# Full-row second products in two attentions, and an SSM's output products grouped by rows

## The chip, the cores and the metric

The kernel runs on one core of one Trainium2 chip, as one program with one launch. The metric is the device time of an execution in microseconds. Before the change it is 1551.39 us, the median of three runs from 1551.03 to 1553.93. A measurement of this kernel can tell apart some 0.2%.

The core has five engines with a queue each: TensorE (PE in the profile, its weight loads apart as PEld), VectorE (DVE), ScalarE (ACT), GpSimd (POOL) and SyncE (SP, which here only starts transfers). Each runs its instructions in the order in which they were issued and waits at an instruction until the semaphores of its operands are there.

## The reference, cut to what matters

Two transformer-like blocks run on one sequence of 512 tokens with 1024 channels, in float32. Block 1 has NSA attention (8 heads of 64, two groups of keys), MLA attention and an MLP, all modulated by a vector c. Block 2 has a state space model (SSM) on 512 channels, a second attention of 8 heads of 64 on the other 512, and a gated MLP.

The change touches three places of it:

```python
# NSA, selected and windowed keys; chunked_attention has the same product
s = jnp.einsum('bghqd,bgqkd->bghqk', qq, k_sel).astype(jnp.float32) * scale - slopes * dist_s[:, :, None]
p = masked_softmax(s, smask[:, :, None])
...
scores = jnp.einsum('bnqhd,bnkhd->bhnqk', qc, kb).astype(jnp.float32) / math.sqrt(HEAD_DIM)
...
# SSM
_, states = lax.associative_scan(combine, (a, bu), axis=1)
y = jnp.einsum('bsgp,ghp->bsgh', states, c_mat).real + d_skip.astype(f32) * uf
```

Scores are sums over 64 head channels. SSM outputs are sums over 64 complex states of each of 32 groups.

## The kernel before, in words

**Order of the work.** The program isn't issued as it is written. `Rec` records every instruction of every engine with what it reads and writes (so every instruction has the source line 337, and names of tiles tell them apart). `Plan.schedule` (line 159) then plays the program through with estimated costs from `Plan.price` (line 121): each engine takes the instruction of the lowest number whose operands are there and for whose tiles there is a place. The order of planned starts is the order issued. For a float32r matmul the price is its columns over 2400 us (line 140); the rows it uses don't enter. `merge` runs several generators side by side by their costs, and each `yield` gives the cost of what was just recorded.

**Stages around the change.** NSA (`nsa_units`, from line 1527) is merged with the dense products of block 1's other inputs (line 1576). Later, `ssm(0)` is merged with dense products of block 2 (line 2053), and then `att2_stream`, `ssm(1)` and further dense products are merged (line 2054). Dense products have names like `mm<-hh,wh`: inputs and weights are each split into a high and a low float32r part, and three products (high-high, low-high, high-low) make one of full accuracy.

**Scores.** `Unit.qk` (class at line 1256) makes the scores of one head and one block of 128 queries, with 128, 256, 384 or 512 keys. `passes` gives two products that accumulate in one bank of PSUM. The first takes `qA` (128 rows: the high part of the query on 64 partitions, its low part on the other 64; even and odd heads have them the other way round) against `kA` (the high part of the key on both halves). The second takes the high part of the query alone, 64 rows, against the low part of the key:

```python
return [(qA[:, cs], kA[:, :n]), (qA[r:r + 64, cs], kL[r:r + 64, :n])]
```

It stands in line 1548 for NSA and in line 2027 for the second attention. NSA's `kL` is written on both halves of its partitions (`kskw`, line 786). In the second attention one tile `k2l` (line 1118, in `qk2_evac`) holds the low keys of two heads, one on each half. MLA has products with 96 rows, which the change doesn't touch.

**The SSM's outputs.** `ssm(hf)` (line 1905) treats half of the SSM's channels. It loads tables `rec` and inputs `U`, makes state products (`T<-U,rec`, 64 columns of the array each), rotates and scans on VectorE and GpSimd, which gives `st` (tiles `ss`: real and imaginary states), and then makes the outputs in lines 1961 to 1973. For each of two sets `o` and each half `e` of the partitions, four groups `k` have three float32 products that accumulate in `Y`: one with `U` (128 rows), one with the real and one with the imaginary states (`T<-ss,rec`, 64 rows, on the lower or the upper half of the partitions by `e`). The three follow each other, group by group. `Y` is a tile of the tag T, which has two places in PSUM (line 501); attention transposes use the same tag.

## Time and profile before

| What | Value |
|---|---|
| median of the runs | 1551.39 us (1551.03 to 1553.93) |
| profiled execution, first to last instruction | 1547.8 us (the profile has no other time of this execution) |
| TensorE busy | 1473.4 us, 95% of the span, 7008 records |
| TensorE weight loads busy | 1193.4 us, 77% |
| VectorE busy | 994.4 us, 64% |
| ScalarE busy | 627.0 us, 41% |
| GpSimd busy | 273.6 us, 18% |
| mean granted clock of TensorE | 0.970 |
| products `S<-kL,qA` / `S<-k2l,qA` / `T<-ss,rec`, 64 rows | 64 / 32 / 128 records |

How to read the profile: one execution is recorded on the chip. "A<-B,C" means an instruction that writes tile A and reads B and C, without buffer numbers; a shape like 64*128 ahead of the sizes is the rows and columns of TensorE's array that a product uses. Float32 products appear as two records each. Busy time of TensorE is the union of its matmuls, whose ends are modelled, so a busy TensorE need not be a fast one; the steps between starts tell more. The granted clock is the share of full speed that TensorE was given. The chain of waits is followed back from the last instruction to what released each step.

### The profile page before, as it was taken

To read this page: it belongs to the slowest core of one execution; us is meant where nothing else is said; L and a number is where in the kernel's file an instruction comes from. 1 tells how busy PE (TensorE), PEld (TensorE's weight loads), DVE (VectorE), ACT (ScalarE), POOL (GpSimd) and SP (SyncE) were. 2 spreads that over 40 slices of the span, in tenths; PEclk is the share of its full clock that TensorE was granted. 3 is DMA by queue.
4 is the path that set the end of the run, shared out by engine and by line. 5 is a ranking of instruction groups with operands and counts; after the bars stand their busy time and mean duration, and the time that the engine had idled before them with its cause. 6 is when DMAs were issued, how large, how long until landed. Compare 5 with 4: busy or idle time off the path is not lost.

```text
span 1547.8 us, 19040 instructions
## 1 busy us (share of the span) xinstructions
PE 1473.4 (95%) x7008; PEld 1193.4 (77%) x7008; DVE 994.4 (64%) x1972; ACT 627.0 (41%) x1057; POOL 273.6 (18%) x262
## 2 busy tenths in 40 slices
PE   4889999998899999999999998999899999999997
PEld 3687777786688888887787887877688888888885
DVE  7835687877997788766443556296876544553544
ACT  3425556665654342332323431274733322231222
POOL 7514040535200000000213111037031000000000
PEclk9998999999999999999999998699899999999998
DMA  9355252434026422333444665113122333333311
GB/s 368 110 181 173 68 168 84 137 109 170 28 94 202 128 76 89 109 105 126 132 146 160 218 225 109 41 56 116 51 93 82 97 108 90 101 95 110 104 60 55
DMA packets 72604, 184.75 MB, mean 119 GB/s; under 512 B 16792, under 2 KB 17640, under 8 KB 72512
## 3 DMA queue, kind: packets, MB, share of 16 engines
q1 hardware_dynamic: 63424, 158.62, 32.2%
q0 software_dynamic: 7552, 22.97, 4.4%
q10 hardware_dynamic: 1536, 1.95, 0.4%
q8 instruction: 55, 0.90, 0.2%
q14 instruction: 37, 0.30, 0.1%
HBM read 165.41 MB, written 19.67 MB: 120 GB/s over the span
## 4 chain that ended last, share of the span: by engine, by line
PE 78%; DVE 9%; issue 5%; DMA 4%; POOL 2%; ACT 2%; SPq 0%; DVEq 0%; POOLq 0%; ACTq 0%
PE mm L337 64%; PE T L337 7%; PE S L337 4%; PE O L337 3%; DVE sb L337 2%; DMA aw<-in_w_ada 2%; POOL aacg L337 1%; DMA adaw<-in_w_ada 1%; DVE wl L337 1%; DVE pl L337 1%; DVE zqd L337 1%; DMA U<-ud 1%; DVE q L337 1%; DVE sr L337 1%; DVE xt L337 0%
## 5 line engine op out<-in xcount | busy, mean ns | idle before, releaser
L337 PE MATMUL mm<-hh,wh 128*128 128x512 f32 x880 | 363.4, 415 | 13.3 <-ACT hh L337 5.8
L337 ACT CAST wh<-wr 128x1024 fp32r<-128x1024 f32 x209 | 219.2, 1051 | 366.1 <-PE mm L337 331.0
L337 PE MATMUL mm<-hl,wh 128*128 128x512 f32 x880 | 355.1, 403 | 0.2 <-DVE hl L337 0.2
L337 PE MATMUL mm<-hh,wl 128*128 128x512 f32 x880 | 352.8, 401 | 0.5 <-DVE wl L337 0.5
L337 DVE TENSOR_TENSOR wl<-wr,wh 128x1024 fp32r<-128x1024 f32 x199 | 256.3, 1289 | 144.8 <-ACT wh L337 142.3
L337 PEld LDWEIGHTS mm<-hh,wh 128*128 128x128 f32 x880 | 167.9, 192 | 52.6 <-ACT hh L337 6.6
L337 PEld LDWEIGHTS mm<-hh,wl 128*128 128x128 f32 x880 | 168.8, 192 | 37.7 <-issue 1.4
L337 PEld LDWEIGHTS mm<-hl,wh 128*128 128x128 f32 x880 | 169.2, 192 | 34.7 <-issue 2.4
L337 PE MATMUL mm<-fh,wl 128*128 128x512 f32 x416 | 162.5, 391 | 0.0
L337 PE MATMUL mm<-fl,wh 128*128 128x512 f32 x416 | 162.3, 390 | 0.0
L337 PE MATMUL mm<-fh,wh 128*128 128x512 f32 x416 | 161.7, 390 | 0.0
L337 PEld LDWEIGHTS mm<-fh,wh 128*128 128x128 f32 x416 | 78.1, 188 | 16.8 <-issue 0.6
L337 PEld LDWEIGHTS mm<-fh,wl 128*128 128x128 f32 x416 | 78.1, 188 | 16.8 <-issue 0.6
L337 PEld LDWEIGHTS mm<-fl,wh 128*128 128x128 f32 x416 | 78.1, 188 | 16.6 <-DVE PBr L337 0.2
L337 ACT ACTIVATE sb<-sb,st 128x256 f32<-128x256 f32 (+3 forms) x128 | 71.5, 560 | 47.4 <-DVE st L337 46.5
L337 POOL TENSOR_TENSOR adacc<-adacc,adaw 128x1024 f32<-128x1024 f32 x28 | 68.9, 2460 | 55.1 <-ACT adaw L337 54.6
L337 PE MATMUL T<-ident,sb 128*128 128x128 f32 x320 | 57.7, 280 | 11.1 <-DVE sb L337 6.0
L337 DVE TENSOR_TENSOR pl<-T,ph 128x384 fp32r<-128x384 f32 (+1 forms) x96 | 56.9, 595 | 16.5 <-ACT ph L337 13.6
L337 ACT CAST ph<-T 128x384 fp32r<-128x384 f32 (+1 forms) x96 | 49.0, 511 | 44.9 <-PE T L337 35.6
L337 POOL TENSOR_TENSOR st<-st,mhalf 128x1 f32<-128x1 f32 x4 | 2.2, 547 | 358.2 <-DVE st L337 358.2
L337 PEld LDWEIGHTS T<-ident,sb 128*128 128x128 f32 x320 | 40.3, 143 | 22.8 <-DVE pl L337 6.2
L337 DVE CUSTOM_DVE_ANT_0 sb<-S,nb 128x256 f32<-128x256 f32 (+2 forms) x96 | 45.3, 482 | 15.6 <-PE S L337 15.0
(373 smaller groups left out, 2560.4 us busy)
## 6 DMA issues: line engine op xcount, KB each, us to landing
wr<-in_w_fc SPq DMA_DIRECT2D x64, 512.0 KB, 3.6
wr<-in_w_in SPq DMA_DIRECT2D x48, 512.0 KB, 4.4
wr<-in_w_gu SPq DMA_DIRECT2D x44, 512.0 KB, 3.6
adaw<-in_w_ada POOLq DMA_DIRECT2D x32, 512.0 KB, 4.3
wr<-in_w_down SPq DMA_DIRECT2D x22, 512.0 KB, 3.5
aw<-in_w_ada SPq DMA_DIRECT2D x32, 256.0 KB, 6.0
wr<-in_w_out SPq DMA_DIRECT2D x16, 512.0 KB, 3.8
rec<-srec SPq DMA_DIRECT2D x28, 256.0 KB, 5.8
```

Source lines behind the costliest of these rows:

```text
L337: fn(*o.a, **o.kw)
```

## The change

The second score products of NSA and of the second attention use all 128 rows: `qA[:, cs]` against the whole `kL`. In NSA both halves of `kL` hold the key's low part, so the query's low part is now multiplied with it too. In the second attention each head gets a `k2l` tile of its own, whose other half is set to zero by GpSimd.

In `ssm`, both `Y` tiles of a set are made first. All eight products with `U` come first, then the products with the states, which alternate between the two halves of the partitions for each `k` and each of the real and imaginary parts. The first product with `U` in a bank now carries the start flag alone. Both copies to `ye` come at the end of the set. The costs that are yielded change from 0.65 per three products to 0.9 per four. Comments and docstrings of the file are gone too.

```diff
@@ qk2_evac
-                kl = slot(F32R, "k2l")
                 for e in range(2):
-                    kA = slot(F32R, "k2A")
+                    kA, kl = slot(F32R, "k2A"), slot(F32R, "k2l")
                     r, o = e * 64, (1 - e) * 64
+                    gp.memset(f(kl)[o:o + 64], 0.0)
                     act.copy(kA[r:r + 64], p[r:r + 64])
                     act.copy(kA[o:o + 64], p[r:r + 64])
                     later(dve.tensor_tensor, kl[r:r + 64], p[r:r + 64], f(kA)[r:r + 64], op=OP.subtract)
@@ nsa_units, and in the same way att2_units
-                    return [(qA[:, cs], kA[:, :n]), (qA[r:r + 64, cs], kL[r:r + 64, :n])]
+                    return [(qA[:, cs], kA[:, :n]), (qA[:, cs], kL[:, :n])]
@@ ssm
         for o in range(2):
             pcr, pci = rec[8 + o], rec[10 + o]
             sr, si = st[o]
+            Y = [bank("T")[:, 0:256].rearrange("p (g c) -> p g c", g=4) for e in range(2)]
             for e in range(2):
-                Y = bank("T")[:, 0:256].rearrange("p (g c) -> p g c", g=4)
-                r = slice(64 * e, 64 * e + 64)
                 for k in range(4):
                     g = 2 * k + e
-                    mm(Y[:, k], rec[2 * o + g // 4][:, 128 * (g % 4):128 * (g % 4) + 128], U[:, 8 * o + g], True, False)
-                    mm(Y[:, k], pcr[r, 128 * k:128 * k + 128], sr[r, k], False, False)
-                    mm(Y[:, k], pci[r, 128 * k:128 * k + 128], si[r, k], False, True)
-                    yield 0.65
-                act.copy(ye[:, 8 * o + e:8 * o + 8:2], Y)
+                    mm(Y[e][:, k], rec[2 * o + g // 4][:, 128 * (g % 4):128 * (g % 4) + 128], U[:, 8 * o + g], k == 0,
+                       False)
+                yield 0.9
+            for k in range(4):
+                for w, (pc, s_) in enumerate(((pcr, sr), (pci, si))):
+                    for e in range(2):
+                        r = slice(64 * e, 64 * e + 64)
+                        mm(Y[e][:, k], pc[r, 128 * k:128 * k + 128], s_[r, k], False, w == 1)
+                yield 0.9
+            for e in range(2):
+                act.copy(ye[:, 8 * o + e:8 * o + 8:2], Y[e])
```

TensorE's order is the same in both kernels up to SSM half 0, so in NSA only the rows of the second products change. In SSM half 0 the order before was this, behind the first wait for the states (`T_1898` and `T_1902` are the two banks, `ss` the states, `rec` the tables; each row is one product):

```order
L337 MATMUL T_1898<-ss_1883,rec_1867 128x64
L337 MATMUL mm_1896<-hh_1804,wh_1886 128x512
L337 MATMUL T_1898<-ss_1883,rec_1869 128x64
L337 MATMUL T_1898<-U_1873,rec_1859 128x64
L337 MATMUL T_1898<-ss_1883,rec_1867 128x64
L337 MATMUL T_1898<-ss_1883,rec_1869 128x64
L337 MATMUL T_1898<-U_1873,rec_1860 128x64
L337 MATMUL T_1898<-ss_1883,rec_1867 128x64
L337 MATMUL T_1898<-ss_1883,rec_1869 128x64
```

Now it is this at the same place (banks `T_1898` and `T_1899`):

```order
L337 MATMUL T_1899<-U_1873,rec_1859 128x64 x2
L337 MATMUL T_1899<-U_1873,rec_1860 128x64 x2
L337 MATMUL T_1899<-ss_1883,rec_1867 128x64
L337 MATMUL T_1899<-ss_1883,rec_1869 128x64
L337 MATMUL T_1898<-ss_1883,rec_1867 128x64
L337 MATMUL T_1899<-ss_1883,rec_1867 128x64
L337 MATMUL T_1898<-ss_1883,rec_1869 128x64
L337 MATMUL T_1899<-ss_1883,rec_1869 128x64
L337 MATMUL T_1898<-ss_1883,rec_1867 128x64
L337 MATMUL T_1899<-ss_1883,rec_1867 128x64
```

The products with `U` moved together ahead of those with the states, which stand in groups of one to ten between dense products; TensorE's whole order has 33 separate stretches of `T<-ss,rec` before (17 in half 0, 16 in half 1) and 17 now (7 and 10). In the second attention before, TensorE's order at the first head is:

```order
L337 MATMUL S_1928<-k2A_1916,qA_1906 128x512
L337 MATMUL S_1947<-k2A_1916,qA_1906 128x384
L337 MATMUL S_1950<-k2A_1916,qA_1906 128x256
L337 MATMUL mm_1946<-hh_1804,wh_1909 128x512
L337 MATMUL S_1928<-k2l_1915,qA_1906 128x512
L337 MATMUL S_1947<-k2l_1915,qA_1906 128x384
L337 MATMUL S_1950<-k2l_1915,qA_1906 128x256
L337 MATMUL mm_1946<-hl_1805,wh_1909 128x512
```

This piece didn't move; in the whole order the 32 products with `k2l` stand in 24 separate stretches before. On POOL the first two new clears stand here, between the clears of the SSM's state tiles (`ss`) and the bias tiles of the second attention (`nb`):

```order
L337 MEMSET ss_1883 128x512
L337 MEMSET ss_1894 128x512
L337 MEMSET k2l_1916 64x512
L337 MEMSET k2l_1918 64x512
L337 DMA nb_1415_1927<-es 128x256
L337 TENSOR_SCALAR nb_1415_1927<-vec 128x256
```

The other six stand further on, among the bias tiles and the rotations of SSM half 1. Four loads of `x2` for the next stage stand later in SP's order than before, among its weight loads.

## The prediction

> **What bounds the kernel now.** I read the page's chain first, then busy time by stage, then the chain inside each stage, then TensorE's timeline.

> ```profile
> PE 78%; DVE 9%; issue 5%; DMA 4%; POOL 2%; ACT 2%; SPq 0%; DVEq 0%; POOLq 0%; ACTq 0%
> ```

> TensorE makes 78% of the chain that ended last, so its time is the kernel's time wherever no other engine ends the wait. Busy time in the stages that the change touches (columns: stretch, its length, then PE, PEld, DVE, ACT, POOL with busy us and instructions, granted clock, DMA share, GB/s): NSA, SSM half 0, the second attention in two parts, its tail.

> ```profile
> 133.00:330.00 197.00, 193.83 (x933) 145.85 (x933) 148.41 (x357) 116.28 (x244) 59.76 (x47) 0.98 0.36 118
> 958.00:997.00 39.00, 38.35 (x124) 31.68 (x125) 9.82 (x25) 3.66 (x7) 2.04 (x3) 0.52 0.03 7
> 997.00:1045.00 48.00, 46.54 (x310) 37.36 (x309) 43.50 (x124) 34.07 (x72) 12.71 (x18) 1.00 0.26 75
> 1045.00:1100.00 55.00, 55.00 (x286) 43.40 (x284) 38.39 (x94) 27.99 (x59) 26.96 (x18) 1.00 0.36 115
> 1100.00:1117.00 17.00, 12.66 (x45) 9.78 (x46) 13.35 (x29) 14.15 (x29) 0.00 (x0) 0.70 0.00 0
> ```

> TensorE fills the first four. VectorE is nearly idle in SSM half 0, busy for three quarters of NSA, and close behind TensorE in 997 to 1045. No single engine fills the tail after 1100. The chain inside 133 to 330, 1000 to 1045 and 1045 to 1100, in this order:

> ```profile
> by line: PE mm L337 42.9%; PE S L337 16.6%; DVE sb L337 9.6%; PE T L337 9.2%; PE O L337 7.4%; issue 4.8%; DVE wl L337 2.4%; DVE pl L337 2.0%; ACT adaw L337 1.1%; ACT sb L337 0.9%; DVE onl L337 0.7%; DVE o L337 0.7%; DVE st L337 0.6%; ACT wh
> by line: PE mm L337 42.8%; PE S L337 15.9%; PE T L337 13.3%; DVE sr L337 8.2%; PE O L337 4.0%; DVE pl L337 3.8%; DVE qA L337 3.1%; DVE wl L337 2.7%; ACT ph L337 2.2%; DVE st L337 1.6%; DVE qk L337 1.3%; issue 0.8%; DVE sb L337 0.6%; ACTq L3
> by line: PE mm L337 51.1%; PE T L337 27.6%; PE S L337 12.8%; PE O L337 7.7%; ACT ph L337 0.9%; issue 0.0%
> ```

> TensorE's share is 42.9 + 16.6 + 9.2 + 7.4 = 76% in NSA, again 76% in the first part of the second attention, and 99% in its second part. I use these shares as the part of a TensorE saving that reaches the end.

> **What a 64-row product costs now.** Matmuls overlap, so a price is the step from one start to the next, not the duration. Two places in NSA (start, duration, instruction, rows * columns of the array):

> ```profile
> 299.87 0.28 PE L337 MATMUL S<-kA,qA 128*128 128x256 f32 x1
> 300.08 0.38 PE L337 MATMUL S<-kL,qA 64*128 64x256 f32 x1
> 300.39 0.50 PE L337 MATMUL mm<-hh,wh 128*128 128x512 f32 x1
> 300.73 0.40 PE L337 MATMUL mm<-hl,wh 128*128 128x512 f32 x1
> 300.96 0.39 PE L337 MATMUL mm<-hh,wl 128*128 128x512 f32 x1
> ...
> 303.72 0.22 PE L337 MATMUL S<-kA,qA 128*128 128x128 f32 x1
> 303.87 0.32 PE L337 MATMUL S<-kL,qA 64*128 64x128 f32 x1
> 304.12 0.50 PE L337 MATMUL mm<-hh,wh 128*128 128x512 f32 x1
> 304.46 0.40 PE L337 MATMUL mm<-hl,wh 128*128 128x512 f32 x1
> 304.70 0.39 PE L337 MATMUL mm<-hh,wl 128*128 128x512 f32 x1
> ```

> For comparison MLA's score products, which use 96 rows, and the weight loads of all 64 kL products:

> ```profile
> 384.52 0.28 PE L337 MATMUL S<-kmH,qml 96*128 96x256 f32 x1
> 384.64 0.28 PE L337 MATMUL S<-kmL,qmh 96*128 96x256 f32 x1
> 384.76 0.40 PE L337 MATMUL mm<-ch,wh 128*128 128x512 f32 x1
> L337 PEld LDWEIGHTS S<-kL,qA 64*128 64x128 f32 x64 | 12.0, 188 | 15.9 <-issue 15.0
> ```

> An undisturbed step is 0.12 us after 256 columns (384.52 to 384.64 to 384.76) and 0.23 us after 512 (300.73 to 300.96). Around kL three steps are long: into it 0.21 for 0.12, out of it 0.31 for 0.12, and the next dense step 0.34 for 0.23. From 299.87 to 300.96 that is 1.09 us where 0.12 + 0.12 + 0.23 + 0.23 = 0.70 would do: 0.39 us lost. At 128 columns, 303.72 to 304.70 takes 0.98 us where 0.11 + 0.11 + 0.23 + 0.23 = 0.68 would do (0.11 from the small products below): 0.30 lost. The load queue idles 15.9 us ahead of the 64 loads of kL, for nothing that is recorded: these loads don't run ahead. Products with 96 rows lose nothing. So it is the passage between half the array's rows and all of them that costs, not a short product as such.

> [...]

> **The sum.** *NSA scores.* 64 second products become full-row products like their kA partners. kL already holds the low part on both halves of its partitions, so nothing is added. At 0.37 us each (between 0.30 and 0.39, near the upper since three of four widths are 256 or more), 64 x 0.37 = 23.7 us of TensorE; by the 76% share 18 us. Bounds: 12, half of it, if VectorE's 148 us bind earlier; 24 if all of it counts.

> *Second attention.* 32 products; where three k2l products stand together they share a passage, so the order of TensorE's instructions has 24 passages: 24 x 0.37 = 8.9 us, half of it before 1045 (4.4 x 76% = 3.4), half after (4.4, less what falls near the tail: 4.0). Together 7.4, bounds 3 and 8.9. Added are four tiles and eight clears of 64x512 on POOL. The nearest clears, of 128x512:

> ```profile
> L337 POOL MEMSET ss<- x4: 522/526/528, 860.1 to 963.5; 128x512 f32 x4
> ```

> 8 x 0.53 = 4.2 us on an engine busy for 12.7 of 48 and 27 of 55 us. Queued behind them on POOL are the bias tiles and the SSM's rotations, and VectorE waits for both; the first two clears stand right behind two of the clears of this row, long before the attention. I take nothing, since POOL's own idle time covers them; uncovered they cost at most 4.2.

> *SSM output products.* Every fp32 product is two records. Half 1 runs at full clock in a regular period, and small full-row products stand early in the program:

> ```profile
> 1052.53 0.50 PE L337 MATMUL mm<-hh,wh 128*128 128x512 f32 x1
> 1052.86 0.39 PE L337 MATMUL mm<-hl,wh 128*128 128x512 f32 x1
> 1053.09 0.40 PE L337 MATMUL mm<-hh,wl 128*128 128x512 f32 x1
> 1053.33 0.33 PE L337 MATMUL T<-U,rec 128*128 128x64 f32 x2
> 1053.59 0.66 PE L337 MATMUL T<-ss,rec 64*128 64x64 f32 x4
> 1054.18 0.53 PE L337 MATMUL mm<-hh,wh 128*128 128x512 f32 x1
> ...
> 97.77 4.74 PE L337 MATMUL S<-fm,wr 128*128 128x62 f32 x41
> 102.34 0.61 PE L337 MATMUL S<-hs,vec 128*128 128x62 f32 x4
> ```

> Undisturbed records of that size step at (102.34 - 97.77) / 41 = 0.111 us. The period of 1.65 us should then be 3 x 0.23 + 6 x 0.111 = 1.36: a visit to 64 rows costs 0.29. Half 1 makes 16 visits, in the new order 10: 6 x 0.29 = 1.7 us. Half 0 runs at half clock (0.52 above):

> ```profile
> 958.65 0.43 PE L337 MATMUL T<-ss,rec 64*128 64x64 f32 x2 [3.94 <-DVE ss L337]
> 960.54 1.11 PE L337 MATMUL T<-ss,rec 64*128 64x64 f32 x4
> 962.20 1.11 PE L337 MATMUL T<-ss,rec 64*128 64x64 f32 x4
> 992.08 0.79 PE L337 MATMUL mm<-hh,wh 128*128 128x512 f32 x1
> ```

> One group takes 962.20 - 960.54 = 1.66 us; six records at half clock should take 6 x 0.222 = 1.33, so a visit costs 0.33. 17 visits become 7: 3.3 us. (Three U products move ahead of the wait of 3.94 us and three dense products behind it; 6 x 0.222 against 3 x 0.43 us, no difference.) That is one bound: ss records one after the other, as now. The new order alternates upper and lower 64 rows, with a bank for each. The nearest rows for such alternation are the state products, which alternate between column halves, at half clock:

> ```profile
> 946.69 3.29 PE L337 MATMUL T<-U,rec 128*64 128x64 f32 x64 [3.20 <-DMA U<-ud]
> 946.00:949.40 3.40, 2.71 (x51) 2.74 (x53) 0.70 (x3) 0.00 (x0) 0.00 (x0) 0.50 1.40 149
> ```

> These step at 3.29 / 64 = 0.051 us, a quarter of 0.222, where half would follow from their half-sized loads: the two halves overlap. If row halves overlap likewise, the 64 ss records of a half cost half: 64 x 0.111 = 7.1 us less in half 0, 3.6 less in half 1. So half 0 saves 3.3 to 10.4 and half 1 saves 1.7 to 5.3. I take the middle, 7 and 3.5: the state products are the nearest case, but only in columns and with half-sized loads. TensorE alone is busy in half 0, so all of it counts.

> [...]

> A cost of the grouping: each set now holds both T banks from its first to its last product, and the next head's transposes stand 12 dense products later in half 1: 12 x 0.23 = 2.8 us late. By the last dense product both orders have done the same work, so I take 0, bound 2.8.

> Sum: 18 + 7.4 + 7 + 3.5 = 36 us. The profiled execution's span of 1547.8 us becomes 1512; the median of the runs lies 3.6 us above that span (1551.4), so 1515.

> **The rivals.** *Larger gain, the clock returns.* Half 0 is at half clock from 960 to 997 although TensorE is busy throughout; full clock returned only after dense products stood alone (from 992.08). If the row halves overlap, the array is used twice as densely and the clock may return after some 8 us; of 33.4 - 10.4 = 23 us the remaining 15 would halve. 18 + 7.4 + 10.4 + 7.5 + 5.3 = 49: 1503. Against it: three dense products in each period did not bring it back before.
> [...]

> *VectorE takes over.* It is already 9.6% of NSA's chain with sb alone, and 43.5 of 48 us busy in the second attention. NSA 12, attention 3, SSM 3.3 + 1.7: 20 us, 1531. Against it: NSA would still need 197 - 24 = 173 us of TensorE for 148 of VectorE.

> *The passage isn't what costs.* If the lost time belonged to the switch of weights between kA and kL, the products would stay as dear: 1551. The 96-row rows speak against it.

> *Slower: the clock falls in the attentions.* A faster TensorE waits more for softmax, as in the tail, where the clock is 0.70. Work at half clock takes twice as long, so 80 us of NSA spent at half clock would lose 40, more than the 36 won, and give 1555. It decides once NSA's mean clock falls below about 0.8. Against it: 0.98 now, and TensorE would remain the busiest engine.

> **How the numbers follow.** My case 0.59; the clock returns 0.22; VectorE takes over 0.12; no passage cost 0.04; slower 0.03. The predicted time is my case's, 1515. Its bounds are 12 + 3 + 3.3 + 1.7 - 2.8 = 17 us (1534) and 24 + 8.9 + 10.4 + 5.3 = 49 us (1503); towards the returning clock I go on to 1497, and stop at 1533 above. What a measurement of this kernel can tell from no change is about 0.2%, 3 us. Faster by more: 0.93 (the first three cases); within: 0.04; slower: 0.03.

> **What would show it.** Right: no idle of the load queue ahead of kL and k2l; steps of 0.12 and 0.23 around them; NSA shorter by about 18 us; half 0 shorter by 3 to 10 at a clock near 0.5; half 1's ss records stepping at 0.11 or 0.056. Wrong: the same long steps around full-row kL; TensorE idle behind VectorE sb or pl in NSA for more than 10 us beyond now; the clock below 0.9 in NSA; attention transposes of half 1 that end its dense work later.

## The result, and the profile after

The changed kernel takes 1514.88 us, the median of four executions (1511.93 to 1517.28), against 1551.21 us for the kernel before. The ratio is 0.9766 with a 95% interval of 0.9740 to 0.9792: faster by some 36 us, as forecast (1515, from 1497 to 1533). The profiled execution has a span of 1515.5 us and a time of 1517.28 us.

The first two lines are from the page of the changed kernel, its busy times and its chain by engine. The others are busy times by stage (columns as in the prediction): a piece of NSA, SSM half 0, the second attention in two parts, its tail.

```profile
PE 1432.6 (95%) x7008; PEld 1179.6 (78%) x7008; DVE 993.3 (66%) x1972; ACT 627.0 (41%) x1057; POOL 280.1 (18%) x270
PE 73%; DVE 13%; issue 5%; DMA 3%; POOL 3%; ACT 2%; DVEq 0%; SPq 0%; ACTq 0%; POOLq 0%
...
140.00:312.00 172.00, 163.41 (x902) 138.06 (x902) 141.19 (x346) 109.79 (x235) 57.94 (x45) 0.99 0.42 132
942.00:976.00 34.00, 34.00 (x141) 27.04 (x142) 11.52 (x27) 6.46 (x12) 2.04 (x3) 0.57 0.09 24
976.00:1014.00 38.00, 35.60 (x275) 31.10 (x274) 37.28 (x113) 29.73 (x66) 14.57 (x21) 1.00 0.27 79
1014.00:1067.00 53.00, 50.63 (x300) 39.75 (x299) 43.88 (x97) 29.08 (x62) 29.52 (x18) 1.00 0.36 110
1067.00:1085.00 18.00, 14.34 (x50) 11.02 (x50) 14.72 (x37) 14.83 (x30) 0.00 (x0) 0.62 0.10 29
```

TensorE's busy time fell by 41 us (1473.4 to 1432.6), and its part of the chain from 78% to 73%; VectorE's rose from 9% to 13%. NSA's clock held (0.99). Half 0 is at half clock for most of its time still (0.57). In 976 to 1014 VectorE is now busy for longer than TensorE.

To compare stages I cut each trace at the starts of the same products: NSA from the first `S<-kA` to the last `O<-pl,VV`, half 0 from the first `T<-ss` to the first `S<-k2A`, the second attention (with SSM half 1 beside it) from there to the last `O<-pl,V`. All in us:

| Stage | Before | After | Gain | Predicted |
|---|---|---|---|---|
| NSA | 205.2 | 186.8 | 18.4 | 18 |
| SSM half 0 | 42.7 | 33.9 | 8.8 | 7 |
| Second attention with SSM half 1 | 111.0 | 104.4 | 6.6 | 7.4 + 3.5 |
| All else | 1188.9 | 1190.4 | -1.5 | 0 |
| Span | 1547.8 | 1515.5 | 32.3 | 36 |

The steps around the full-row products, in NSA (start, duration, instruction), and the weight loads of all 64 `kL` and all 32 `k2l` products:

```profile
302.07 0.34 PE L337 MATMUL S<-kA,qA 128*128 128x384 f32 x1
302.24 0.34 PE L337 MATMUL S<-kL,qA 128*128 128x384 f32 x1
302.42 0.39 PE L337 MATMUL O<-pch,VC 128*128 128x512 f32 x1
...
303.35 0.28 PE L337 MATMUL S<-kA,qA 128*128 128x256 f32 x1
303.46 0.28 PE L337 MATMUL S<-kL,qA 128*128 128x256 f32 x1
303.58 0.40 PE L337 MATMUL mm<-hh,wh 128*128 128x512 f32 x1
...
L337 PEld LDWEIGHTS S<-kL,qA 128*128 128x128 f32 x64 | 12.2, 191 | 1.9
L337 PEld LDWEIGHTS S<-k2l,qA 128*128 128x128 f32 x32 | 5.9, 188 | 0.6
```

The product of 256 keys now steps 0.11 us into `kL` and 0.12 us out of it, where it was 0.21 and 0.31. The load queue's idle time ahead of `kL` went from 15.9 to 1.9 us.

The SSM's products in half 1 at full clock, then in half 0 at half clock:

```profile
1019.45 0.40 PE L337 MATMUL mm<-hh,wl 128*128 128x512 f32 x1
1019.77 0.66 PE L337 MATMUL T<-ss,rec 64*128 64x64 f32 x8
1020.36 0.50 PE L337 MATMUL mm<-hh,wh 128*128 128x512 f32 x1
...
950.91 1.12 PE L337 MATMUL T<-ss,rec 64*128 64x64 f32 x8
951.96 0.79 PE L337 MATMUL mm<-hh,wh 128*128 128x512 f32 x1
```

Eight records with states take 0.59 us from their start to the next product (1019.77 to 1020.36). Before, four took the same (1053.59 to 1054.18). At half clock eight last 1.12 us, where four lasted 1.11. So products of the upper and the lower rows overlap wholly.

### The profile page after: what moved, and what is told of

Its sections match the earlier page's. It is cut to its first block, busy times and chain, and to the rows that moved or that the text cites. A ratio compares the mean times of both kernels' runs of the same rounds, so it can differ in the third digit from the quotient of the medians.

```text
span 1515.5 us, 19052 instructions
## 1 busy us (share of the span) xinstructions
PE 1432.6 (95%) x7008; PEld 1179.6 (78%) x7008; DVE 993.3 (66%) x1972; ACT 627.0 (41%) x1057; POOL 280.1 (18%) x270
## 3 DMA queue, kind: packets, MB, share of 16 engines
q1 hardware_dynamic: 63424, 158.62, 33.4%
## 4 chain that ended last, share of the span: by engine, by line
PE 73%; DVE 13%; issue 5%; DMA 3%; POOL 3%; ACT 2%; DVEq 0%; SPq 0%; ACTq 0%; POOLq 0%
PE mm L337 62%; PE T L337 5%; DVE sb L337 4%; PE S L337 3%; PE O L337 3%; POOL aacg L337 3%; DMA adaw<-in_w_ada 1%; DVE wl L337 1%; DVE pl L337 1%; DVE sr L337 1%; DVE q L337 1%; ACT wh L337 1%; DVE zqd L337 1%; DVE o L337 0%; DVE st L337 0%
## 5 line engine op out<-in xcount | busy, mean ns | idle before, releaser
L337 PE MATMUL mm<-hh,wh 128*128 128x512 f32 x880 | 359.9, 411 | 13.0 <-ACT hh L337 4.5
L337 ACT CAST wh<-wr 128x1024 fp32r<-128x1024 f32 x209 | 219.7, 1053 | 361.8 <-PE mm L337 325.1
L337 PE MATMUL mm<-hl,wh 128*128 128x512 f32 x880 | 353.2, 401 | 0.6 <-DVE hl L337 0.6
L337 PE MATMUL mm<-hh,wl 128*128 128x512 f32 x880 | 351.4, 400 | 0.5 <-DVE wl L337 0.5
L337 DVE TENSOR_TENSOR wl<-wr,wh 128x1024 fp32r<-128x1024 f32 x199 | 251.9, 1267 | 139.2 <-ACT wh L337 137.6
L337 PEld LDWEIGHTS mm<-hh,wh 128*128 128x128 f32 x880 | 168.0, 192 | 46.7 <-ACT hh L337 5.5
L337 PEld LDWEIGHTS mm<-hh,wl 128*128 128x128 f32 x880 | 168.4, 191 | 36.6 <-DVE wl L337 1.3
L337 PEld LDWEIGHTS mm<-hl,wh 128*128 128x128 f32 x880 | 168.7, 192 | 33.8 <-DVE hl L337 2.5
L337 PE MATMUL mm<-fh,wl 128*128 128x512 f32 x416 | 162.5, 391 | 0.0
L337 PE MATMUL mm<-fl,wh 128*128 128x512 f32 x416 | 162.3, 390 | 0.0
L337 PE MATMUL mm<-fh,wh 128*128 128x512 f32 x416 | 161.7, 390 | 0.0
L337 PEld LDWEIGHTS mm<-fh,wl 128*128 128x128 f32 x416 | 78.1, 188 | 16.9 <-issue 0.6
L337 PEld LDWEIGHTS mm<-fh,wh 128*128 128x128 f32 x416 | 78.1, 188 | 16.8 <-issue 0.6
L337 PEld LDWEIGHTS mm<-fl,wh 128*128 128x128 f32 x416 | 78.1, 188 | 16.4 <-DVE PBr L337 0.2
L337 ACT ACTIVATE sb<-sb,st 128x128 f32<-128x128 f32 (+3 forms) x128 | 71.8, 562 | 42.4 <-DVE st L337 41.6
L337 POOL TENSOR_TENSOR adacc<-adacc,adaw 128x1024 f32<-128x1024 f32 x28 | 69.6, 2485 | 52.5 <-ACT adaw L337 52.0
L337 PE MATMUL T<-ident,sb 128*128 128x128 f32 x320 | 59.0, 285 | 19.0 <-DVE pl L337 10.7
L337 POOL TENSOR_TENSOR st<-st,mhalf 128x1 f32<-128x1 f32 x4 | 2.2, 546 | 358.3 <-DVE st L337 358.3
L337 PEld LDWEIGHTS T<-ident,sb 128*128 128x128 f32 x320 | 40.5, 145 | 32.8 <-issue 13.8
L337 DVE TENSOR_TENSOR pl<-T,ph 128x384 fp32r<-128x384 f32 (+1 forms) x96 | 57.1, 595 | 11.2 <-ACT ph L337 9.3
L337 ACT CAST ph<-T 128x384 fp32r<-128x384 f32 (+1 forms) x96 | 48.9, 512 | 34.9 <-PE T L337 29.4
L337 DVE TENSOR_TENSOR swg<-mm,R 128x512 f32<-128x512 f32 x21 | 14.5, 691 | 61.2 <-PE mm L337 61.2
```

The source lines that it names most:

```text
L337: fn(*o.a, **o.kw)
```

## The experiments

Theory T, as in the prediction: each visit of a 64-row product among full-row products costs TensorE 0.3 to 0.4 us, and row halves overlap. Rivals: the parts need each other; VectorE takes the second attention over; the overlap is worth nothing; the clock, by coming back or not, decides half 0.

### Each part alone

NSA's line alone, in the kernel before:

```diff
-                    return [(qA[:, cs], kA[:, :n]), (qA[r:r + 64, cs], kL[r:r + 64, :n])]
+                    return [(qA[:, cs], kA[:, :n]), (qA[:, cs], kL[:, :n])]
```

> The kernel before with NSA's change alone. Passage theory (each visit of a 64-row product costs 0.30 to 0.39 us of TensorE, 76% of it on the chain): about 18 us faster, near 1533; NSA 187 us instead of 205, SSM half 0 and the second attention as before (42.7 and 111 us). Rival, the three parts of the change need each other (one frees an engine for the next): less than 15 us here, and the parts alone do not add up to the 36 us of the whole change.

1531.32 us, ratio 0.9895 (0.9877 to 0.9912): 16 us faster. NSA takes 188.8 us, half 0 42.4, the second attention 110.9. T holds, and the gain in NSA needs nothing else.

The second attention alone: its scores over full rows, a `k2l` tile for each head, the clears.

```diff
-                kl = slot(F32R, "k2l")
                 for e in range(2):
-                    kA = slot(F32R, "k2A")
+                    kA, kl = slot(F32R, "k2A"), slot(F32R, "k2l")
                     r, o = e * 64, (1 - e) * 64
+                    gp.memset(f(kl)[o:o + 64], 0.0)
...
-                return [(qA[:, cs], kA[:, :n]), (qA[r:r + 64, cs], kL[r:r + 64, :n])]
+                return [(qA[:, cs], kA[:, :n]), (qA[:, cs], kL[:, :n])]
```

> The kernel before with the second attention's change alone. As predicted, 24 visits at 0.37 us with most of it on the chain: 7.4 us faster, near 1544. Rival, VectorE holds the chain in this stage once the visits are gone (after the whole change its steps are some 43% of the chain from 976 to 1014 us): about 3 us faster, near 1548. The clears on GpSimd cost 0 by both; if they cost, up to 4.2 us more.

1543.60 us, ratio 0.9967 (0.9955 to 0.9978): 5 us faster, and the stage 106.0 us where it was 111.0. The gain lies halfway between the two that were forecast (7.4 and 3). The chain inside the stage, first before (1001 to 1112), then with this part alone (1000 to 1108), then with the whole change (976 to 1080):

```profile
by line: PE mm L337 41.2%; PE T L337 20.2%; PE S L337 12.8%; PE O L337 8.8%; DVE sr L337 3.3%; ACT ph L337 2.8%; ACT yy L337 1.8%; DVE pl L337 1.6%; DVE qA L337 1.2%; DVE wl L337 1.1%; ACT ot L337 1.0%; issue 1.0%; ACT yq L337 0.9%; ACT sb 
```

```profile
by line: PE mm L337 25.7%; PE T L337 14.9%; DVE sb L337 8.8%; PE S L337 7.1%; PE O L337 4.8%; DVE pl L337 4.7%; issue 3.4%; DVE sr L337 3.3%; ACT ph L337 2.8%; ACT sb L337 2.6%; DVE qA L337 2.5%; ACT yq L337 2.0%; DVE st L337 1.9%; ACT yy L
```

```profile
by line: PE mm L337 17.3%; DVE sb L337 15.2%; DVE pl L337 8.0%; PE T L337 6.5%; issue 5.8%; DVE wl L337 4.9%; DVE k2l L337 4.7%; DVE o L337 3.6%; DVE sr L337 3.3%; PE O L337 3.1%; DMA wr<-in_w_out 2.9%; PE S L337 2.7%; DVE qA L337 2.7%; DVE
```

TensorE's four entries go from 83% to 53% to 30%: with each saving VectorE ends more of the waits. The chain of the kernel before could not show this: a share tells who ends the wait now, and not who stands close behind.

The SSM's new order alone (the last part of the diff shown above):

> The kernel before with the SSM's new order alone. Half 0 shorter by about 9 us (42.7 to 34) by both theories. If half 1 gives the predicted 3.5: 12 us faster in all, near 1539. If the attention beside half 1 is bound by VectorE: 9 us, near 1542. If the T banks' longer holding costs (bound 2.8 us): 6 us, near 1545.

1539.11 us, ratio 0.9940 (0.9920 to 0.9960): 9 us faster. Half 0 takes 33.0 us, a gain of 9.8. The stage with half 1 takes 112.3 us, longer by 1.3, though its products with states overlap as above. This execution has 10 us at half clock in a part of the stage where the three whose chains stand above have none:

```profile
1011.00:1021.00 10.00, 10.00 (x35) 7.54 (x34) 9.84 (x33) 7.42 (x20) 3.23 (x6) 0.51 0.06 15
```

In all the stage has 14.8 us at half clock here, against 6.0 in the kernel before; work at half clock takes about twice as long (in the kernel before a dense step takes 0.43 us instead of 0.23, a record with states 0.21 instead of 0.11), so the 8.8 us more are some 4 us of time (an estimate). Without them the stage would have been about 3 us shorter than before, near the predicted 3.5; that is an estimate, and half 1's gain is not shown by itself. The three ratios add to 10.5 + 3.3 + 6.0 = 19.8 thousandths, 31 us, against 36 for the whole change; by their intervals (about 4 us each way) the two don't differ. Against the second measurement of the whole change, further below, 41 us, they fall short by 10. Some 6 of these lie in half 0 (33.0 us here, 26.8 in that trace), where full clock came back earlier.

### Is it the passage that costs?

The kernel before, with NSA's scores of 384 and 512 keys in two pieces each, so that full-row and 64-row products change places half as often again:

```diff
-                    return [(qA[:, cs], kA[:, :n]), (qA[r:r + 64, cs], kL[r:r + 64, :n])]
+                    return [x for u, v in (((0, n),) if n < 384 else ((0, 256), (256, n))) for x in ((qA[:, cs], kA[:, u:v], u, v), (qA[r:r + 64, cs], kL[r:r + 64, u:v], u, v))]
...
```

(left out: `Unit.qk` makes each pair in its own columns `u` to `v` of the bank)

> The kernel before, with NSA's scores of 384 and 512 keys made in two pieces (256 + 128 and 256 + 256), so that full-row and 64-row products alternate twice as often there: 96 visits instead of 64, the same rows and columns. Theory (a visit costs 0.39 us at 256 and 0.30 at 128 columns): 16 x 0.39 + 16 x 0.30 = 11 us more of TensorE and 2 us for the smaller pieces, 76% of it on the chain: NSA 10 us longer, 206 to 216, near 1559. Rival (the cost belongs to the 64 rows, or is a fixed one for each product whatever its neighbours): 2 to 5 us, near 1553.

1562.81 us, ratio 1.0090 (1.0067 to 1.0113): 13 to 14 us slower. NSA takes 222.7 us, 16 more than the mean of four traces with the old products (206.6). Two pieces of a 512-key score:

```profile
309.14 0.39 PE L337 MATMUL mm<-hh,wl 128*128 128x512 f32 x1
309.38 0.28 PE L337 MATMUL S<-kA,qA 128*128 128x256 f32 x1
309.58 0.38 PE L337 MATMUL S<-kL,qA 64*128 64x256 f32 x1
309.89 0.38 PE L337 MATMUL S<-kA,qA 128*128 128x256 f32 x1
310.21 0.38 PE L337 MATMUL S<-kL,qA 64*128 64x256 f32 x1
310.52 0.50 PE L337 MATMUL mm<-hh,wh 128*128 128x512 f32 x1
310.86 0.40 PE L337 MATMUL mm<-hl,wh 128*128 128x512 f32 x1
311.09 0.28 PE L337 MATMUL S<-kA,qA 128*128 128x256 f32 x1
```

From one `kL` to the next, 309.58 to 310.21, it takes 0.63 us where two steps of 0.12 would do: 0.39 us lost, just the price that the prediction read. The `kA` product between two `kL` products is full-row and yet steps 0.32 instead of 0.12. That is a cost of the change of form, not of the 64 rows, and the rival of 2 to 5 us falls. The stage lost more than my 10 us, but not all of it to the visits: it spent 20.5 us at half clock, where the four with the old products spent 6.8 to 10.2. The 11 us more are some 5 us of time (an estimate), which leaves 10 to 11 for the visits, as forecast.

### What the overlap is worth

The whole change, but the products with states one half after the other:

```diff
-            for k in range(4):
-                for w, (pc, s_) in enumerate(((pcr, sr), (pci, si))):
-                    for e in range(2):
-                        r = slice(64 * e, 64 * e + 64)
+            for e in range(2):
+                r = slice(64 * e, 64 * e + 64)
+                for k in range(4):
+                    for w, (pc, s_) in enumerate(((pcr, sr), (pci, si))):
                         mm(Y[e][:, k], pc[r, 128 * k:128 * k + 128], s_[r, k], False, w == 1)
-                yield 0.9
+                    if k % 2: yield 0.9
```

> The whole change, but the products with the states are issued one half of the partitions after the other, so that upper and lower rows no longer alternate; the grouping and the number of visits (19 for 17) stay. Theory (row halves overlap, and this was most of half 0's gain): half 0 longer by 5 to 7 us than with the whole change (64 records of 0.111 us that ran beside others), half 1 by 0 to 3.6; near 1520 to 1525. Rival, the fewer visits brought the gain and alternation nothing: half 0 the same 34 us, 1515 to 1516.

1510.82 us (1507.48 to 1523.19), ratio 0.9767 (0.9738 to 0.9796): by its time no different from the whole change, and below both forecasts. The trace is that of the slowest execution. Its rows at half clock, beside those of the whole change above:

```profile
951.51 1.97 PE L337 MATMUL T<-ss,rec 64*128 64x64 f32 x8
953.41 0.79 PE L337 MATMUL mm<-hh,wh 128*128 128x512 f32 x1
```

Eight records take 1.90 us and not 1.05, and half 0 takes 38.9 us instead of 33.9. So the overlap is worth 5 us there, as T has it; why the median did not show them was open. I ran the same kernel again, with the changed kernel beside it.

> The changed kernel itself once more, as the base for the other runs of this group. 1511 to 1516; SSM half 0 takes 33 to 34 us at a clock of 0.5.

1506.38 us (1502.72 to 1514.29), ratio 0.9733 (0.9708 to 0.9758). That is below the 1511 to 1516 that I had expected, and this execution has a half 0 of 26.8 us instead of 33 to 34:

```profile
936.00:950.00 14.00, 13.86 (x59) 11.48 (x60) 5.96 (x20) 0.65 (x2) 2.05 (x3) 0.51 0.05 19
950.00:963.00 13.00, 13.00 (x82) 10.25 (x81) 5.65 (x7) 5.64 (x9) 0.00 (x0) 1.00 0.21 52
```

The clock comes back at 950, 13.7 us after it fell. It is the same program as the execution above, in which half clock lasted for 30.7 us. Another chip is not the whole reason: the kernel of the last experiment below has the same order on TensorE in half 0 and ran on this chip, and there it lasted for 27.3 us.

> The kernel without alternation once more: its executions had gone from 1507.5 to 1523.2, and the profiled one was the slowest of them, with half 0 at 38.9 us and half clock. Theory (the clock comes back earlier in half 0 in some executions of this order, since its products follow each other instead of overlapping): an execution near 1507 has half 0 at full clock for a good part and takes 30 us or less there; one near 1521 has it at 0.5 throughout; median 1507 to 1513. Rival (the spread comes from elsewhere): half 0 takes 39 us again whatever the execution's time, and the difference to the changed kernel lies in another stage.

1511.84 us (1508.87 to 1524.23), ratio 0.9767 (0.9738 to 0.9797). Half clock lasts 13.7 us here too, and half 0 takes 29.6 us, against 26.8 for the order with overlap: 2.8 us apart. The clock does come back early in some executions of this order, but not because its products follow each other: with overlap it did the same. By these four executions the overlap is worth 5.0 us where half clock lasts and 2.8 where it ends early. Between executions the clock moves half 0 by 7 to 9 us (33.9 and 26.8, 38.9 and 29.6), which is more.

### What decides the clock

In all 14 traces of this study the granted clock is either full or half and changes on a grid of 3.41 us. In half 0 the half clock lasted for so many of these stretches: 11 in each of four kernels with the old order (37.5 us); 9, 8, 8 and 4 with the new order; 10 and 4 without overlap. For every stretch I worked out how much of the array was used: the time in which columns stream, times the share of the array's rows and columns that the product uses. I counted 0.23 us per 512 columns at full clock, as the dense steps show, 0.456 at half clock, an assumed doubling (dense steps there are 0.43, so that a stretch of them counts 1.07), and twice as much for float32 records, transposes among them. That factor is an assumption that fits these stretches: in the kernel before, transposes of 128 columns step at 0.11 us, 1.9 times as much per column as the dense steps, but records of 62 columns step at 0.11 too. Between 920 and 1110 us:

| Clock in the stretch | Use of the array | Clock after it |
|---|---|---|
| full | below 0.37 | fell in 37 of 37 |
| full | 0.37 to 0.43 | fell in 7 of 16 |
| full | above 0.43 | fell in 0 of 571 |
| half | below 0.74 | came back in 0 of 102 |
| half | 0.74 to 0.84 | came back in 7 of 19 |
| half | above 0.84 | came back in 36 of 36 |

In half 0 the old order uses 0.27 to 0.68 of the array until its dense products stand alone. The new one uses 0.61 to 0.73 from its second stretch on in the first execution, just under the bound. In the one that came back early a stretch reaches 0.77; that the place of the grid against the program decides this is argued, not shown, and with the SSM's order alone 0.77 and 0.78 did not suffice.

In work done the two bounds are one. At full clock 0.37 to 0.43 of the array, and at half clock 0.74 to 0.84, both come to some 5.5 to 6.4 products of 512 columns over the whole array in 3.41 us. At half clock the same mix does less of them in a stretch, so a mix may keep full clock and yet not win it back: the new order kept it at 0.51 to 0.69 of the array in one execution (with the splits on VectorE, further below). These bounds were read off the stretches of the table. In the 3200 stretches from 135 to 915 us of the same traces, off which nothing was read, half clock followed all 44 with less than 5 such products, 32 of 104 with 5 to 6.5, and none of 3052 with more. Whether the share of the columns counts is open: without it the best single bound has 12 of the table's stretches on the wrong side instead of 10, and 3 of these 3200 instead of 20.

In the kernel before, TensorE is busy for all of the 37.00 us from 959 to 996, at a mean clock of 0.51, so it takes more than a TensorE without a gap to bring the clock back. Use of the array fits the stretches of the table.

One test of what lets the clock fall: a scan on VectorE was priced at 0.136 us by the planner, while the first eight in half 0 take 0.74 each. With the right price more dense products stand ahead of the states.

```diff
-            return 0.069 + n / 960.0
+            return 0.72 if name == "tensor_tensor_scan" else 0.069 + n / 960.0
```

> The whole change, with one price of the planner altered: a scan on VectorE counts 0.72 us (as measured) and not 0.136. TensorE then has 21 dense products instead of 6 between the first products with U and the wait for the first states: 15 x 0.23 = 3.5 us more work, as long as TensorE now idles there (3.45 us). Theory (that idle time lets the clock fall, and half 0 then stays at half clock): TensorE doesn't idle, the clock stays at 1.0 and half 0's 34 us lose 10 to 15: near 1501 to 1505. Rival (the small products themselves let the clock fall): the clock is 0.5 again a few us later, 1509 to 1515.

1506.62 us (1502.49 to 1513.22), ratio 0.9727 (0.9701 to 0.9753): as the changed kernel beside it (1506.38), and in neither forecast. TensorE's idle time is gone (0.49 us), but the clock fell all the same one stretch later, among the small products, and came back after 13.7 us. Half 0 takes 23.6 us, and the stage behind it 112.2 instead of 103 to 104. It has 18.4 us at half clock there, against 9.9 in the execution beside it; that explains some 4 us of the difference, and the rest is open (the new price moves half 1's work too). The rival was right that idle time isn't needed; what an undisturbed half 0 is worth stayed open.

### Why the scans are slow

In the changed kernel (VectorE's scans of the first set and of the second, GpSimd, and TensorE's wait):

```profile
933.95 5.91 DVE L337 TENSOR_TENSOR_SCAN sr<-rho,sr 128x64 f32<-128x64 f32 x8
943.74 1.56 DVE L337 TENSOR_TENSOR_SCAN sr<-rho,sr 128x64 f32<-128x64 f32 x8
...
934.25 4.73 POOL L337 TENSOR_TENSOR wl<-wr,wh 128x1024 fp32r<-128x1024 f32 x2 [14.30 <-DMA U<-ud]
...
941.88 0.68 PE L337 MATMUL T<-ss,rec 64*128 64x64 f32 x2 [3.45 <-DVE ss L337]
```

The same eight scans take 5.91 us beside two weight splits of GpSimd and 1.56 us without. Of the eight, two last 2.46 and 2.41 us, one beside each split (2.40 and 2.38 us), and six last 0.26 to 0.29. The two long ones start 0.09 and 0.11 us behind their splits and end 0.15 and 0.14 us after them. So a scan that starts behind a split ends only when the split has ended; what holds it the trace doesn't show. For the test the two splits went to VectorE, which the planner puts behind the scans:

```diff
+    W.on_gp = False
     go(merge([(ssm(0), 36.0), (run(j_att2), 20.8)]))
+    W.on_gp = True
```

> The whole change, with the two weight splits (wl, 128x1024) that GpSimd made in SSM half 0 now on VectorE, behind its scans. In the runs so far the eight scans of the first set take 5.9 us where they lie beside these splits and the eight of the second set 1.56 us. Theory (the splits slow the scans, TensorE idles 3 us for the first states, the clock falls, and whether it comes back during half 0 is chance): the first scans take about 1.6 us, TensorE idles under 1.5 us, no half clock from there to the attention; half 0 takes 17 to 21 us instead of 27 to 34, and the time is near 1498, with less spread. Rival (the scans are slow for another reason, or the small products let the clock fall on their own): scans 5.9 us or half clock again, 1506 to 1515.

1500.84 us (1492.06 to 1509.31), ratio 0.9691 (0.9654 to 0.9728). Its scans, its wait, and half 0:

```profile
932.44 1.56 DVE L337 TENSOR_TENSOR_SCAN sr<-rho,sr 128x64 f32<-128x64 f32 x8
...
937.03 0.43 PE L337 MATMUL T<-ss,rec 64*128 64x64 f32 x2 [0.29 <-DVE ss L337]
...
937.00:958.00 21.00, 20.64 (x140) 16.56 (x141) 13.68 (x24) 6.42 (x12) 4.51 (x5) 1.00 0.32 84
```

The theory holds for this execution: scans 1.56 us, a wait of 0.29 us, full clock, half 0 in 20.8 us. (The planner's order in half 0 shifts a little with the splits, so the scans are not all that changed.) The promise of less spread failed: three of six executions lie above 1505. The same two lines in the kernel before:

> The kernel before with the same move of the two weight splits and nothing else. It tells what the SSM's new order is worth when the clock does not fall. If the clock stays (theory): half 0 takes 22 to 26 us instead of 42.7 and the time is near 1530. If the old order's single 64-row products let it fall without any idle time (its windows then use too little of the array): half 0 38 to 42 us, 1544 to 1549.

1544.28 us, ratio 0.9966 (0.9953 to 0.9979): 5 us faster, and half 0 takes 39.7 us, nine stretches of it at half clock, as forecast for a clock that falls without idle time. TensorE around the fall, at 962.7:

```profile
958.83 0.39 PE L337 MATMUL mm<-hl,wh 128*128 128x512 f32 x1
959.14 0.66 PE L337 MATMUL T<-ss,rec 64*128 64x64 f32 x4
959.73 0.43 PE L337 MATMUL T<-U,rec 128*128 128x64 f32 x2
960.10 0.66 PE L337 MATMUL T<-ss,rec 64*128 64x64 f32 x4
960.68 0.43 PE L337 MATMUL T<-U,rec 128*128 128x64 f32 x2
...
962.58 0.69 PE L337 MATMUL mm<-hh,wl 128*128 128x512 f32 x1
963.07 0.53 PE L337 MATMUL T<-U,rec 128*128 128x64 f32 x2
963.52 1.11 PE L337 MATMUL T<-ss,rec 64*128 64x64 f32 x4
```

TensorE has no idle time here, and yet the clock falls: the stretch from 959.3 uses 0.27 of the array by the reckoning above. With the old order the clock falls even without a wait; with the new one TensorE can keep it. So, by one execution each, the new order is worth 42.7 - 33.9 = 8.8 us at half clock, and 39.7 - 20.8 = 19 us where the scans are free and the clock holds.

At last, output products of half 0 spread among the dense ones, with the splits on VectorE:

```diff
-                yield 0.9
+                yield 0.9 if hf else 1.6
```

(in both places of the new order)

> As the kernel with the splits on VectorE, and in SSM half 0 each group of four output products is priced 1.6 instead of 0.9, so that three to nine dense products stand between any two groups (before: none to three, and 29 dense products in one run at the end). Theory (the clock falls where a 3.4 us stretch uses less than some 0.36 of the array's rows and time, and this mix leaves none): no half clock in half 0 in any execution; median 1494 to 1498, the slowest below 1505. Rival (what makes some executions of that kernel slow lies elsewhere, or more switches between forms cost more): median 1500 to 1505, some executions above 1505.

1502.75 us (1498.63 to 1503.14), ratio 0.9692 (0.9671 to 0.9712). The profiled execution has no half clock in half 0, and none of the five lies above 1503.2: the theory foresaw this steadiness. But the median isn't lower. In the trace the second attention takes 107.4 us instead of 102.4, with 14.0 us at half clock (one stretch of it from 995.6) instead of 8.9; that explains about half of the 5 us, and the rest is open. Both versions with the splits on VectorE stand below the kernel before by 47 to 48 us and below the changed kernel's two medians by 4 to 14; against the better of these two (0.9733) the intervals still touch.

### Stores in NSA

After the change NSA's chain has an entry for the gate tiles' stores, for whose places other tiles wait (first the changed kernel, then with the edit; 171 us of NSA each):

```diff
-                t = slot(F32, "tg")
+                t = early("tg")
```

> The whole change, with NSA's gate tiles (written by ScalarE, stored to memory, never read again) in the pool of early tiles, so that no tile of the attention waits for a store to land. After the change two stores make 7.1% of NSA's chain, 12 us, where they ended no long wait before. Theory (a new wait that the faster TensorE ran into): NSA 4 to 8 us shorter, near 1507 to 1511. Rival (VectorE or the next wait stands right behind): 0 to 2 us, 1512 to 1515.

```profile
by line: PE mm L337 34.5%; DVE sb L337 10.7%; PE S L337 9.7%; PE T L337 7.9%; PE O L337 6.6%; issue 5.5%; DMA sig_b<-tg 3.8%; DMA sig_a<-tg 3.3%; DVE wl L337 2.8%; DVE pl L337 2.4%; DVE smc L337 2.4%; ACT sb L337 1.9%; ACT wh L337 1.8%; ACT
```

```profile
by line: PE mm L337 38.5%; DVE sb L337 12.8%; PE S L337 11.4%; PE T L337 9.6%; PE O L337 7.9%; issue 3.8%; DVE wl L337 3.6%; DVE smc L337 2.4%; ACT adaw L337 1.9%; DVE pl L337 1.7%; ACT wh L337 1.1%; ACT sb L337 1.0%; DVE Pc L337 0.8%; DVE 
```

1508.83 us, ratio 0.9745 (0.9716 to 0.9775). The number lies in the theory's range, but the changed kernel beside it took 1506.38. The stores are gone from the chain, and NSA takes 189.6 us, no less than in the other traces with the new products (186.8 to 189.4). So the rival was right about the stage: TensorE and VectorE take over the chain, and an entry of 7% was worth nothing.

## Why the prediction was right, and where not

- **The price of a visit** (0.39 us at 256 columns, from three long steps) is shown: the steps fell to 0.11 and 0.12, and an added visit costs 0.39 us.
- **NSA, 64 x 0.37 x 76% = 18**: 18.4 in the profiled pair, and 18.1 between the means of four traces with the old products (206.6) and nine with the new (188.5). The share of 76% fits this stage, where 18.1 of 23.7 us is 76%, and the added visits with some 10 to 11 of 13; it is no rule, as the second attention shows.
- **SSM half 0, 7 (3.3 to 10.4)**: 8.8, and 9.8 alone, where half clock lasted for most of the stage. The mechanism held; "I take the middle" was too cautious, since the row halves overlap wholly (at half clock eight records last 1.12 us, where four lasted 1.11), as I had read it of the column halves of the nearest row. The serial order shows 5 us of it.
- **Second attention 7.4 and half 1 3.5**: 6.6 together in the profiled pair, and 7.7 between the means of four traces with this stage as it was before (111.3) and three with the whole change in it (103.6). This is the mis-sized term. The step that failed is "I use these shares as the part of a TensorE saving that reaches the end" for the second attention: 99% in its second part was a share from before the saving. TensorE's busy time in the stage fell by 9.3 us (105.2 to 95.9), and the stage by 6.6. Alone the attention's part gained 5.0. About 2 us of the shortfall can be the clock: the stage has 9.9 us at half clock after the change and 6.0 before. The rival "VectorE takes over" came true in part in this one stage (it had 3 us for the attention), not in NSA.
- **The clears on GpSimd at 0 and the holding of the T banks at 0**: neither was tried alone. The attention's part gained 5.0 us with its clears in it. With the SSM's order alone the stage with half 1 grew by 1.3 us; the half clock there can explain that, but does not exclude a cost of the T banks.
- **Outside the span, 3.6 us**: it is 1.8 us in every execution that shows both its span and its time (1517.28 and 1515.5, for one). I had set a profiled span against a median of other executions. 36 us were forecast and 32 came between the two spans; this term and the spread between executions made the final number look better than the sum. That 1514.88 meets 1515 so closely is luck: measured once more, the same kernel took 1506.38, with a ratio of 0.9733 (41 us). The two medians differ by 0.6%, so the 0.2% that a measurement was to tell apart held for the kernel before and not for this one.
- **"The clock returns", chance 0.22**: it did not in the profiled execution (30.7 us at half clock), and it did in another of the same program (13.7 us). What I took for a choice between two cases differs between executions. No run shows the 8 us that I allowed for it: the shortest half clock in half 0 lasted 13.7. My reason for it, twice as dense a use of the array, fits the table above; my reason against it, that dense products did not bring the clock back before, held for the old order's use of 0.27 to 0.68 only. Half 0 then gained 15.9 us where I had 17.9.
- **"The passage isn't what costs"** falls by the added visits; **"the clock falls in the attentions"** by NSA's 0.99.

## What to carry to other kernels

Price a product by the steps from start to start around it, with both neighbours: a short form among long ones can cost three times its own step (here 0.39 us lost around one of 0.12), and grouping or widening it pays even where it multiplies zeros (5 us in the second attention alone). Use a share of the chain as the part that counts only while the saving is small beside the next engine's slack, and look at the busy times of that stage for who is next. Where a stage runs at half clock though TensorE is busy, count how much of the array its products use, allow for the time at half clock before two traces of a stage are compared, and run a kernel more than once before a difference of some us there is believed.
